# One pool of 62 operand tiles in place of three, and two plain tiles in place of a double one

## The chip, the cores and the metric

The kernel runs on one core of a Trainium2 chip. The metric is the device time of one execution in microseconds (us), lower is better. The core has five engines with a queue each, which run their instructions in order and wait for one another through semaphores: TensorE (PE in the rows, its weight loads PEld), VectorE (DVE), ScalarE (ACT), GpSimd (POOL) and SyncE (SP), which issues most of the loads.

## The reference

A conformer-like block and then two recurrent layers, on one sequence of 512 positions and 1024 channels, in float32:

```python
def first_block(x, ...):
    h = h + 0.5 * swiglu(rms_norm(h, ffn1_norm), ...)       # D_FF = 2816
    u = rms_norm(h, mix_norm); z = u @ w_in
    ya = neighbourhood_attention_2d(qa, ka, va, na_rpb)      # 8 heads of 64
    yb = windowed_gqa_sink(rope(qb), rope(kb), vb, sink)     # 8 heads, 2 for keys and values
    merged = sigmoid(ga) * (ya @ w_branch_a) + sigmoid(gb) * (yb @ w_branch_b)
    h = h + merged @ w_out
    h = h + 0.5 * swiglu(rms_norm(h, ffn2_norm), ...)
    return rms_norm(h, final_norm)

def second_block(x, ...):
    x = x + mlstm_mixer(rmsnorm(x, ln_g[0]), ...)   # 4 heads, causal convolution of 4 taps, output gate
    x = x + rglru_mixer(rmsnorm(x, ln_g[1]), ...)   # width 1536, convolution, gates in 8 blocks, scan
    return rmsnorm(x, final_g)
```

## The kernel before, in words

Channels lie on the 128 partitions and the 512 positions along the free axis, so the state is eight tiles `h` of 128x512. Every float32 matrix is split into a rounded part `hi` and a rest `lo`, and a product is three matmuls into one PSUM bank: hi by hi, hi by lo, lo by hi (`mm3`, L113 to L115). Weights are loaded by `wload`: SP loads `raw`, ScalarE casts it to `hi` (L98), VectorE subtracts to `lo` (L100); five `hi` and five `lo` tiles rotate, so a cast waits until TensorE has done with an older weight. Activations are split by `split` (ScalarE L122, VectorE L124) and the normalised inputs by `operand` (L139, L140).

The stages run one after the other: feed-forward 1, the mixer with its two attentions, feed-forward 2, the mLSTM, the RG-LRU and the last norm. At the start of most stages `opening` makes groups of 24 matmuls from the operands while `sumsq` squares the state on ScalarE (L157) and adds the squares on VectorE (L166); `rstd` (L178, L179) and `rows` (L185, L187) make the row of factors `rb` from it, with which VectorE scales what leaves PSUM (`silu2` L202 and L203, for one).

In the feed-forward, 18 of 22 pairs of hidden blocks go through `pair_products`, a scheme with seven products of half size for a 2 by 2 block product. It gathers its four quarters of 256 columns in a double tile `t` of 128x1024 (L325 to L337), then makes silu times product (L339, L340) and splits it. `xhalves` prepares the sums of the operands, in four steps.

In the mLSTM, for each of four heads, `x_proj` projects and scales, `conv` (L1006, L1009 three times) is followed by silu (L811) and a split, in `x_conv`; `o_proj` makes four groups at once in all four `bank` tiles, which ScalarE empties with a tanh into four `ctile`s (L869); `qk_proj` makes four more groups in `bank` tiles, emptied by L851 and L852. Head 0 also has `gate_rows` (L749 to L784) and `residual` (eight L789 on VectorE, with the row from L187). `scores` begins with four transposes (L878).

In the RG-LRU, four parts of three tiles: `x_proj` (L1043 and a convolution each), `gates` (six groups of 6 or 9 matmuls in `cbank` tiles, emptied by L1065 on ScalarE), `recur` (ScalarE L1076, L1077, L1080 with table loads between; VectorE L1084 to L1088; a split) and `out_proj` (L1096), in an order written at the end of `rglru`.

That order of calls is the program's. The framework's scheduler reorders each engine's instructions by priorities (`tc.high_priority`, with 100 for what empties PSUM and 75 for weights) and by when tiles of a pool are to be had. A pool has a fixed number of buffers under a tag: 40 tiles "act" of 128x512, 18 tiles "chain" (`ctile`) and 2 double tiles "four" in SBUF; 4 "bank" and 4 "cbank" in PSUM. A tile waits for the release of an older one when its pool has none left. The double tiles also hold the rope tables, two gates (`room`) and the `hi` parts of `qk_proj`.

Of the kernel before, what the change touches and what calls it, by code (L numbers as in the profile page):

```python
# [8 lines left out]
F32 = mybir.dt.float32  # L9
F32R = mybir.dt.float32r  # L10
# [4 lines left out]
P = 128  # L15
T = 512
# [26 lines left out]
def kernel(ctx: ExitStack, tc: tile.TileContext, a, out):  # L43
# [2 lines left out]

    cp = ctx.enter_context(tc.tile_pool(name="cp", bufs=1))
    op = ctx.enter_context(tc.tile_pool(name="op", bufs=1))
    ap = ctx.enter_context(tc.tile_pool(name="ap", bufs=40))
    wp = ctx.enter_context(tc.tile_pool(name="wp", bufs=5))  # L50
    sp = ctx.enter_context(tc.tile_pool(name="sp", bufs=32))
    gp = ctx.enter_context(tc.tile_pool(name="gp", bufs=2))
    hp = ctx.enter_context(tc.tile_pool(name="hp", bufs=KD))
    rp = ctx.enter_context(tc.tile_pool(name="rp", bufs=2))
    xp = ctx.enter_context(tc.tile_pool(name="xp", bufs=18))
    vp = ctx.enter_context(tc.tile_pool(name="vp", bufs=5))
    pp = ctx.enter_context(tc.tile_pool(name="pp", bufs=4, space=PSUM))
    qp = ctx.enter_context(tc.tile_pool(name="qp", bufs=4, space=PSUM))
# [1 line left out]
    def act_tile(dt=F32):  # L60
        return ap.tile([P, T], dt, tag="act", name="act")
# [2 lines left out]
        return pp.tile([P, T], F32, tag="bank", name="bank")  # L64

    def ctile(dt=F32):
        return xp.tile([P, T], dt, tag="chain", name="chain")

    def cbank():
        return qp.tile([P, T], F32, tag="cbank", name="cbank")  # L70
# [234 lines left out]
    def pair_products(pair, b, nxt, between):  # L305
        w = pair.w
        if nxt:
            nxt.load()
        m = bank()
        product(m[:, L], w["a11"], b["b11"])  # L310
        p1 = ctile()
        with tc.high_priority(offset=EVAC):
            S.copy(p1[:, L], m[:, L])
        c1, c2 = cbank(), cbank()
        product(c1[:, L], w["a12"], b["b21"])
        if nxt:
            nxt.first()
        between(0)
        product(c2[:, L], w["s1"], b["t1"])
        product(c2[:, R], w["s3"], b["t3"])  # L320
        product(c1[:, R], w["s2"], b["t2"])
        t = gp.tile([P, 2 * T], F32, tag="four", name="four")
        v = act_tile()
        with tc.high_priority(offset=EVAC):
            V.tensor_tensor(quarters(t)[:, 0:4:3], quarters(c1), twice(p1[:, L]), op=ALU.add)  # L325
            V.tensor_tensor(quarters(v), quarters(c2), twice(t[:, 3 * HT :]), op=ALU.add)
            V.scalar_tensor_tensor(t[:, 3 * HT :], c2[:, R], 1.0, v[:, L], op0=ALU.mult, op1=ALU.add)
        between(1)
        c3 = bank()
        product(c3[:, L], w["s4"], b["b22"])  # L330
        if nxt:
            nxt.sums()
        product(c3[:, R], w["a22"], b["t4"])
        if nxt:
            nxt.last()
        with tc.high_priority(offset=EVAC):
            V.tensor_tensor(t[:, HT : 3 * HT], c3, v, op=ALU.add)  # L337
        g, u = t[:, :T], t[:, T:]
        S.activation(g, g, AF.Silu)  # L339
        V.scalar_tensor_tensor(u, u, -1.0, g, op0=ALU.mult, op1=ALU.mult)  # L340
        return split(u)

    def ffn(x, gain, gu, dn, pre=None):
        xs = operand(x, gain)
        pre = pre or [wload(gu[0])]
        ws = pre
        pre, _, rb = opening(lambda n: group(ws[n] if n < len(ws) else wload(gu[n]), xs, (bank if n < 2 else cbank)()), x)

        def plain(j):
            pg, pu = pre[2 * j : 2 * j + 2] if j < 2 else [group(wload(gu[2 * j + i]), xs) for i in range(2)]  # L350
            s = silu2(pg, rb)
            u = act_tile()
            with tc.high_priority(offset=EVAC):
                V.tensor_tensor(u, pu, rb, op=ALU.mult)
            V.tensor_tensor(u, u, s, op=ALU.mult)
            return split(u)

        def down(o, w, base, us):
            ps = group(w, us, base=base)
            with tc.high_priority(offset=EVAC):  # L360
                V.scalar_tensor_tensor(x[o], ps, 0.5, x[o], op0=ALU.mult, op1=ALU.add)

        def down_two(o, k0):
            c = slice(k0 * P, k0 * P + T)
            with tc.high_priority(offset=BOOST):
                raw = raw_load([dn[o][:, c], dn[o + 1][:, c]], None)
                return wsplit(raw)

        b, step = xhalves(x, gain, rb)
        pr = [plain(0), plain(1)]  # L370
        for k in range(4):
            step(k)
        pr += [plain(2), plain(3)]
        def down_job(j):

            if j >= 20:
                return lambda i: None
            o, got, us = 2 * (j % 4), [], old

            def step(i):  # L380
                if i < 0:
                    got.append(down_two(o, 4 * (j // 4 - 1)))
                else:
                    down(o + i, got[0], 4 * i, us)

            return step

        cur = Pair(gu[8], gu[9])
        cur.load()
        cur.first()  # L390
        cur.sums()
        cur.last()
        old, new = pr, []
        for j in range(4, KF):
            nxt = Pair(gu[2 * j + 2], gu[2 * j + 3]) if j + 1 < KF else None
            job = down_job(j)
            job(-1)
            new.append(pair_products(cur, b, nxt, job))
            cur = nxt
            if j % 4 == 3 and j < 19:  # L400
                old, new = new, []
        for o in range(KD):
            dw = wload(dn[o][:, 16 * P :], 6 * P)
            down(o, dw, 0, new)
# [4 lines left out]
    def mixer(x):  # L409
# [32 lines left out]
        rope_t = {}  # L442

        def rope_tables():
            both = gp.tile([P, 2 * T], F32, tag="four", name="four")
            for i in range(2):
                t = both[:, i * T : (i + 1) * T]
                S.dma_start(t, a["rope"][i])
                rope_t[i] = t

# [29 lines left out]
            S.copy(vb, pv)  # L480
            bv.append(vb)

        room = []

        def gate(i):
            ps = group(wload(win[i]), xs)
            if i < 20:
                if not room:
                    room.append(gp.tile([P, 2 * T], F32, tag="four", name="four"))
                g = room[0][:, (i - 18) * T : (i - 17) * T]  # L490
            else:
                g = act_tile()
            with tc.high_priority(offset=EVAC):
                V.tensor_tensor(g, ps, rb, op=ALU.mult)
            S.activation(g, g, AF.Tanh, scale=0.5)
            return g
# [211 lines left out]
    def mlstm(x):  # L708
# [128 lines left out]
        def qk_proj(hd):  # L837
            xcs = st[hd].pop("xcs")
            qk = []
            for i in range(2):  # L840
                w = wload(a["mh"][hd][12 + i])
                w3 = tuple(z.rearrange("p (k m) -> p k m", k=4) for z in w)
                both = gp.tile([P, 2 * T], F32R, tag="four", name="four")
                for m in range(2):
                    ps = bank()
                    for k in range(4):
                        mm3(ps, tuple(z[:, k, m * P : (m + 1) * P] for z in w3), xcs[k], k == 0, k == 3)
                    hi, lo = both[:, m * T : (m + 1) * T], act_tile(F32R)
                    scale = (1.0 / 16, 1.0)[i]
                    with tc.high_priority(offset=EVAC):  # L850
                        S.activation(hi, ps, AF.Copy, scale=scale)  # L851
# [416 lines left out]
```

## Time and profile before

| | us |
|---|---|
| three runs | 1811.58, 1811.38, 1811.50 (median 1811.5) |
| the profiled execution | 1811.49 |
| its span | 1809.8 |
| TensorE busy (x9640) | 1786.7, 99% |
| VectorE busy (x1985) | 1244.5, 69% |
| ScalarE busy (x1205) | 813.6, 45% |
| GpSimd busy (x89) | 65.6, 4% |

The span runs from the first to the last instruction of the profile; what the execution's own time has beyond it lies around it. The granted clock of TensorE stands at nine tenths or more in all 40 slices. Busy time of 99% says that TensorE rarely had nothing in it; matmuls are pipelined, so one of 512 columns is shown with 0.39 us although the next starts 0.23 us later.

### The profile page before, as it was taken

What the parts mean: (1) busy time and instruction counts of PE and PEld (TensorE: products, weight loads), DVE (VectorE), ACT (ScalarE), POOL (GpSimd) and SP (SyncE); (2) the same over time, 40 slices, a digit from 0 to 9 for tenths busy, and PEclk for the clock granted to TensorE, in tenths of its full rate; (3) what the DMA queues carried; (4) which work ended last, traced back from release to release, by engine and by line L of the source; (5) the groups of instructions that cost most, each with busy time, mean ns of one, the idle gap of its engine ahead of it and who ended that gap; (6) DMA issues with size and microseconds to landing.
All of it is one profiled execution on the core that took longest, in us unless ns stands there. A gap on an engine that the chain in (4) does not pass through costs nothing.

```text
span 1809.8 us, 24643 instructions
## 1 busy us (share of the span) xinstructions
PE 1786.7 (99%) x9640; PEld 1515.3 (84%) x9640; DVE 1244.5 (69%) x1985; ACT 813.6 (45%) x1205; POOL 65.6 (4%) x89
## 2 busy tenths in 40 slices
PE   8999999999999999999999999999999999999998
PEld 6899999887776688799999988888888888888886
DVE  7977777735656465887777766758366566777775
ACT  5443344524345433443444444535334444456662
POOL 1000000000000000010000000000000000000000
PEclk9999999999999999999999999999999999999999
DMA  7466554433322123265556432222222231322312
GB/s 230 116 165 156 149 155 131 139 105 97 102 82 70 47 94 105 69 176 151 153 152 155 118 109 89 71 93 94 77 93 87 70 105 59 102 91 87 99 61 73
DMA packets 74805, 198.10 MB, mean 109 GB/s; under 512 B 8000, under 2 KB 8128, under 8 KB 74688
## 3 DMA queue, kind: packets, MB, share of 16 engines
q1 hardware_dynamic: 63024, 174.35, 30.0%
q0 software_dynamic: 9792, 18.88, 6.5%
q10 hardware_dynamic: 1872, 3.29, 0.6%
q8 instruction: 76, 1.25, 0.3%
q14 instruction: 41, 0.34, 0.1%
HBM read 193.08 MB, written 2.10 MB: 108 GB/s over the span
## 4 chain that ended last, share of the span: by engine, by line
PE 80%; issue 13%; DVE 4%; ACT 1%; DMA 1%; SPq 0%; POOLq 0%; POOL 0%; ACTq 0%; DVEq 0%
PE bank L113 21%; PE bank L114 20%; PE bank L115 20%; PE cbank L113 5%; PE cbank L115 5%; PE cbank L114 5%; PE cbank L635 1%; PE cbank L603 1%; DVE chain L124 1%; PE cbank L909 1%; PE cbank L910 1%; PE cbank L911 1%; DVE act L273 1%; PE cbank L572 0%; PE cbank L942 0%
## 5 line engine op out<-in xcount | busy, mean ns | idle before, releaser
L113 PE MATMUL bank<-act,hi 128*128 128x512 f32 (+1 forms) x1648 | 615.2, 374 | 8.3 <-ACT act L139 7.0
L114 PE MATMUL bank<-act,hi 128*128 128x512 f32 (+1 forms) x1648 | 612.8, 373 | 1.1 <-DVE act L140 1.0
L115 PE MATMUL bank<-act,lo 128*128 128x512 f32 (+1 forms) x1648 | 611.5, 372 | 0.7 <-DVE lo L100 0.7
L98 ACT CAST hi<-raw 128x1024 fp32r<-128x1024 f32 (+2 forms) x210 | 212.3, 1014 | 424.6 <-PE bank L114 193.7
L113 PEld LDWEIGHTS bank<-act,hi 128*128 128x128 f32 x1648 | 310.7, 189 | 67.0 <-ACT act L139 7.0
L114 PEld LDWEIGHTS bank<-act,hi 128*128 128x128 f32 x1648 | 310.9, 189 | 56.4 <-DVE act L140 3.3
L115 PEld LDWEIGHTS bank<-act,lo 128*128 128x128 f32 x1648 | 310.9, 189 | 56.2 <-issue 1.9
L100 DVE TENSOR_TENSOR lo<-raw,hi 128x1024 fp32r<-128x1024 f32 (+2 forms) x210 | 246.6, 1176 | 100.6 <-ACT hi L98 99.7
L220 ACT CAST hi<-raw 128x1024 fp32r<-128x1024 f32 x140 | 146.2, 1050 | 232.0 <-PE cbank L114 107.8
L222 DVE TENSOR_TENSOR lo<-raw,hi 128x1024 fp32r<-128x1024 f32 x140 | 170.8, 1224 | 82.1 <-ACT hi L220 77.7
L113 PE MATMUL cbank<-chain,hi 128*128 128x256 f32 x432 | 122.3, 283 | 1.7 <-ACT hi L220 1.7
L115 PE MATMUL cbank<-chain,lo 128*128 128x256 f32 x432 | 122.3, 283 | 0.9 <-DVE lo L222 0.9
L114 PE MATMUL cbank<-chain,hi 128*128 128x256 f32 x432 | 122.2, 283 | 0.0
L113 PE MATMUL cbank<-act,hi 128*128 128x256 f32 (+1 forms) x264 | 88.2, 334 | 0.0
L114 PE MATMUL cbank<-act,hi 128*128 128x256 f32 (+1 forms) x264 | 87.6, 332 | 0.0
L115 PE MATMUL cbank<-act,lo 128*128 128x256 f32 (+1 forms) x264 | 87.5, 332 | 0.0
L113 PE MATMUL bank<-hi,act 128*128 128x512 f32 x224 | 87.5, 391 | 0.0
L115 PE MATMUL bank<-hi,act 128*128 128x512 f32 x224 | 87.5, 391 | 0.0
L114 PE MATMUL bank<-lo,act 128*128 128x512 f32 x224 | 87.2, 389 | 0.0
L113 PEld LDWEIGHTS cbank<-chain,hi 128*128 128x128 f32 x432 | 82.7, 192 | 3.5 <-ACT hi L220 2.1
L115 PEld LDWEIGHTS cbank<-chain,lo 128*128 128x128 f32 x432 | 82.7, 192 | 1.4 <-DVE lo L222 1.1
L114 PEld LDWEIGHTS cbank<-chain,hi 128*128 128x128 f32 x432 | 82.8, 192 | 1.2
(287 smaller groups left out, 2574.0 us busy)
## 6 DMA issues: line engine op xcount, KB each, us to landing
raw<-in_mh_dram SPq DMA_DIRECT2D x64, 512.0 KB, 3.4
raw<-in_gu_dram SPq DMA_DIRECT2D x52, 512.0 KB, 3.5
raw<-in_gu_dram SPq DMA_DIRECT2D x72, 256.0 KB, 2.9
raw<-in_gu_dram POOLq DMA_DIRECT2D x36, 512.0 KB, 6.0
raw<-in_win_dram SPq DMA_DIRECT2D x34, 512.0 KB, 3.5
raw<-in_dn_dram SPq DMA_DIRECT2D x64, 256.0 KB, 2.9
v<-in_gu_dram SPq DMA_DIRECT2D x36, 256.0 KB, 2.6
raw<-in_mo_dram SPq DMA_DIRECT2D x16, 512.0 KB, 3.4
```

The costliest lines, as they stand in the source:

```text
L98: S.copy(hi[:, :cols], raw[:, :cols])
L100: V.tensor_tensor(lo[:, :cols], raw[:, :cols], f(hi[:, :cols]), op=ALU.subtract)
L113: PE.matmul(ps, st[0], mv[0], start=start, stop=False)
L114: PE.matmul(ps, st[0], mv[1], start=False, stop=False)
L115: PE.matmul(ps, st[1], mv[0], start=False, stop=stop)
L124: V.tensor_tensor(lo, x, f(hi), op=ALU.subtract)
L220: S.copy(hi, raw)
L222: V.tensor_tensor(lo, raw, f(hi), op=ALU.subtract)
L273: V.scalar_tensor_tensor(t, x[i], gain[:, i : i + 1], rb, op0=ALU.mult, op1=ALU.mult)
L603: PE.matmul(ps[:, :n], bq[i][ro, nb * P : nb * P + P], bk[0][ro, b0 * P : b1 * P], start=True, stop=True)
L635: PE.matmul(po[64 * g : 64 * g + 64, :], bv[0][:, kb * P + 64 * g : kb * P + 64 * g + 64], ptc, start=kb == b0, stop=kb == b1 - 1)
L909: PE.matmul(ps[:, :n], wh, vh[:, c0:c1], start=s == 0, stop=False)
```

## The change

The pools "four" and "chain" are gone; `ctile` takes its tiles from "act", which has 62 buffers (40 + 18 + 2 double ones). `pair_products` writes into two plain tiles `one` and `two`: the strided write to quarters 0 and 3 becomes a plain one into `one`, the last add of 512 columns becomes two of 256, and the silu and the split move into a function `hidden`. The rope tables, the two gates and the `hi` parts of `qk_proj` are plain tiles.

```diff
-    ap = ctx.enter_context(tc.tile_pool(name="ap", bufs=40))
+    ap = ctx.enter_context(tc.tile_pool(name="ap", bufs=62))
-    gp = ctx.enter_context(tc.tile_pool(name="gp", bufs=2))
-    xp = ctx.enter_context(tc.tile_pool(name="xp", bufs=18))
...
     def ctile(dt=F32):
-        return xp.tile([P, T], dt, tag="chain", name="chain")
+        return ap.tile([P, T], dt, tag="act", name="chain")
...
-        t = gp.tile([P, 2 * T], F32, tag="four", name="four")
-        v = act_tile()
+        one, two, v = act_tile(), act_tile(), act_tile()
         with tc.high_priority(offset=EVAC):
-            V.tensor_tensor(quarters(t)[:, 0:4:3], quarters(c1), twice(p1[:, L]), op=ALU.add)
-            V.tensor_tensor(quarters(v), quarters(c2), twice(t[:, 3 * HT :]), op=ALU.add)
-            V.scalar_tensor_tensor(t[:, 3 * HT :], c2[:, R], 1.0, v[:, L], op0=ALU.mult, op1=ALU.add)
+            V.tensor_tensor(quarters(one), quarters(c1), twice(p1[:, L]), op=ALU.add)
+            V.tensor_tensor(quarters(v), quarters(c2), twice(one[:, R]), op=ALU.add)
+            V.scalar_tensor_tensor(two[:, R], c2[:, R], 1.0, v[:, L], op0=ALU.mult, op1=ALU.add)
...
-            V.tensor_tensor(t[:, HT : 3 * HT], c3, v, op=ALU.add)
-        g, u = t[:, :T], t[:, T:]
+            V.tensor_tensor(one[:, R], c3[:, L], v[:, L], op=ALU.add)
+            V.tensor_tensor(two[:, L], c3[:, R], v[:, R], op=ALU.add)
+        return one, two
+
+    def hidden(pair, b, nxt, between):
+        g, u = pair_products(pair, b, nxt, between)
         S.activation(g, g, AF.Silu)
...
-            new.append(pair_products(cur, b, nxt, job))
+            new.append(hidden(cur, b, nxt, job))
...
-            both = gp.tile([P, 2 * T], F32, tag="four", name="four")
             for i in range(2):
-                t = both[:, i * T : (i + 1) * T]
+                t = act_tile()
                 S.dma_start(t, a["rope"][i])
...
-                both = gp.tile([P, 2 * T], F32R, tag="four", name="four")
                 for m in range(2):
...
-                    hi, lo = both[:, m * T : (m + 1) * T], act_tile(F32R)
+                    hi, lo = act_tile(F32R), act_tile(F32R)
```

The change moves instructions, most of them in other functions than those it edits. Three places follow, each as the engine's order before and then in the changed kernel (a line is shown as line, operation, out<-in, shape; x4 is four alike in a row). The changed kernel's lines are lower: L861 is L869 of before, L804 L811, L120 L122, L936 L944, L843 L851, L96 L98, L1057 L1065, L1068 L1076, L1072 L1080, L201 L203, L164 L166, L1088 L1096, L1114 L1122, L176 L178.

ScalarE in head 0 of the mLSTM, before: silu (L811) and split (L122) of the second to fourth convolution, with the four tanh of o_proj (L869).

```order
L811 ACTIVATE act<-act 128x512
L98 CAST hi<-raw 128x1024
L122 CAST act<-act 128x512
L869 ACTIVATE chain<-bank,small 128x512 x2
L944 ACTIVATE act<-act,skq 128x512
L869 ACTIVATE chain<-bank,small 128x512 x2
L811 ACTIVATE act<-act 128x512
L98 CAST hi<-raw 128x1024
L122 CAST act<-act 128x512
L944 ACTIVATE act<-act,skq 128x512
L811 ACTIVATE act<-act 128x512
L122 CAST act<-act 128x512
```

The same in the changed kernel:

```order
L804 ACTIVATE act<-act 128x512
L120 CAST act<-act 128x512
L936 ACTIVATE act<-act,skq 128x512
L804 ACTIVATE act<-act 128x512
L120 CAST act<-act 128x512
L936 ACTIVATE act<-act,skq 128x512
L804 ACTIVATE act<-act 128x512
L120 CAST act<-act 128x512
L861 ACTIVATE chain<-bank,small 128x512 x4
L936 ACTIVATE act<-act,skq 128x512
L843 ACTIVATE act<-bank 128x512
```

The four tanh that stood behind the second split stand behind the fourth. In head 3 they move in the same way, from around the third split to behind the fourth; in heads 1 and 2 they stay.

ScalarE in the RG-LRU, before: from the last L1065 of the first gates through the first recurrence.

```order
L1065 ACTIVATE chain<-cbank,small 128x512
L1076 ACT_TABLE_LOAD
L1076 ACTIVATE chain<-chain,small 128x512 x2
L1077 ACTIVATE chain<-chain,small 128x512 x2
L1076 ACTIVATE chain<-chain,small 128x512
L203 ACT_TABLE_LOAD
L203 ACTIVATE act<-act 128x512
L1077 ACTIVATE chain<-chain,small 128x512
L1080 ACT_TABLE_LOAD
L1080 ACTIVATE chain<-chain 128x512 x3
```

The same in the changed kernel:

```order
L1057 ACTIVATE chain<-cbank,small 128x512
L96 CAST hi<-raw 128x1024
L201 ACTIVATE act<-act 128x512
L96 CAST hi<-raw 128x896
L201 ACTIVATE act<-act 128x512
L96 CAST hi<-raw 128x896
L1068 ACT_TABLE_LOAD
L1068 ACTIVATE chain<-chain,small 128x512
L201 ACT_TABLE_LOAD
L201 ACTIVATE act<-act 128x512
```

Three weight casts and two silu stand ahead of the recurrence now. Further on, the L1065 of the second gates stand behind the three splits of the next convolutions, and on TensorE the last 15 matmuls of those gates behind 90 of the following groups.

VectorE at the end of the kernel, before: L1096 empties the last groups, L1122 scales the state, L166 adds squares, L178 begins the last norm.

```order
L1122 TENSOR_SCALAR act<-h,vec 128x512
L166 TENSOR_TENSOR chain<-chain 128x512
L1096 SCALAR_TENSOR_TENSOR h<-bank,h 128x512
L1122 TENSOR_SCALAR act<-h,vec 128x512
L166 TENSOR_TENSOR chain<-chain 128x512
L1096 SCALAR_TENSOR_TENSOR h<-bank,h 128x512
L1122 TENSOR_SCALAR act<-h,vec 128x512
L178 TENSOR_SCALAR small<-cbank 128x4
```

The same in the changed kernel:

```order
L1114 TENSOR_SCALAR act<-h,vec 128x512
L1088 SCALAR_TENSOR_TENSOR h<-bank,h 128x512
L1114 TENSOR_SCALAR act<-h,vec 128x512
L1088 SCALAR_TENSOR_TENSOR h<-bank,h 128x512
L1114 TENSOR_SCALAR act<-h,vec 128x512
L164 TENSOR_TENSOR chain<-chain 128x512 x6
L176 TENSOR_SCALAR small<-cbank 128x4
```

The six adds that stood one by one between the L1096 now stand together behind the last L1122.

## Rows read from the trace of the kernel before

**Rows 1.** What TensorE waited for, whole span: total us, times, longest.
```profile
PE bank L113 <- ACT act L139: 7.0, 1, 7.0
...
PE bank L478 <- DVE act L475: 1.6, 1, 1.6
PE bank L114 <- DVE act L140: 1.0, 3, 0.5
```

**Rows 2.** Busy us (PE, PEld, DVE, ACT, POOL), PEclk, DMA share, GB/s: pair loops.
```profile
75.00:345.00 270.00, 270.00 (x1861) 252.20 (x1861) 207.25 (x267) 112.95 (x147) 18.11 (x15) 1.00 0.58 154
```

**Rows 3.** Groups by line and shape, VectorE, 100 to 330 us: busy, mean ns.
```profile
L337 DVE TENSOR_TENSOR four<-bank,act 128x512 f32<-128x512 f32 x16 | 10.9, 684 | 0.0
...
L327 DVE SCALAR_TENSOR_TENSOR four<-cbank,act 128x256 f32<-128x256 f32 x16 | 6.8, 424 | 0.5
```

**Rows 4.** Timeline, TensorE, qk_proj of head 0: start, length, then idle before.
```profile
1133.19 0.60 PE L185 MATMUL cbank<-ident,small 128*128 128x128 f32 x4
...
1143.03 1.21 PE L113 MATMUL bank<-act,hi 128*128 128x512 f32 x4 [0.49 <-ACT act L122]
...
1146.63 0.68 PE L113 MATMUL cbank<-four 128*128 128x512 f32 x2 [0.28 <-ACT four L851]
```

**Rows 5.** Timeline, ScalarE, the same place.
```profile
1129.43 0.69 ACT L869 ACTIVATE chain<-bank,small 128x512 f32<-128x512 f32 x1
...
1141.69 0.63 ACT L811 ACTIVATE act<-act 128x512 f32<-128x512 f32 x1 [3.70 <-DVE act L1009]
```

**Rows 6.** Timeline, VectorE, the same place.
```profile
1133.83 0.69 DVE L187 COPY rb<-cbank 128x512 f32<-128x512 f32 x1
1134.56 2.08 DVE L789 SCALAR_TENSOR_TENSOR h<-h,vec,rb 128x512 f32<-128x512 f32 x3
1136.55 0.68 DVE L124 TENSOR_TENSOR act<-act 128x512 fp32r<-128x512 f32 x1
1137.15 0.54 DVE L1006 TENSOR_SCALAR act<-act,vec 128x512 f32<-128x512 f32 x1
...
1145.29 1.21 DVE L100 TENSOR_TENSOR lo<-raw,hi 128x1024 fp32r<-128x1024 f32 x1
```

**Rows 7.** Timelines of VectorE, ScalarE and TensorE, head 3.
```profile
1490.21 2.32 DVE L1009 SCALAR_TENSOR_TENSOR act<-act,vec 128x511 f32<-128x511 f32 x3
...
1493.95 0.62 ACT L122 CAST act<-act 128x512 fp32r<-128x512 f32 x1
...
1491.57 0.39 PE L113 MATMUL bank<-act,hi 128*128 128x512 f32 x1
```

**Rows 8.** Timelines of ScalarE and (last two rows) TensorE, RG-LRU.
```profile
1621.30 1.28 ACT L1076 ACT_TABLE_LOAD   x1
...
1635.92 0.95 ACT L98 CAST hi<-raw 128x896 fp32r<-128x896 f32 x1 [0.33 <-PE bank L114]
...
1662.76 0.68 ACT L1065 ACTIVATE chain<-cbank,small 128x512 f32<-128x512 f32 x1
...
1666.30 0.62 ACT L122 CAST act<-act 128x512 fp32r<-128x512 f32 x1 [0.72 <-DVE act L1009]
...
1687.33 0.62 ACT L122 CAST act<-chain 128x512 fp32r<-128x512 f32 x1 [2.09 <-DVE chain L1088]
...
1658.38 0.39 PE L113 MATMUL cbank<-act,hi 128*128 128x512 f32 x1
...
1700.55 0.39 PE L113 MATMUL cbank<-act,hi 128*128 128x512 f32 x1
```

**Rows 9.** Timelines of VectorE and (third row) TensorE at the end.
```profile
1793.91 0.69 DVE L166 TENSOR_TENSOR chain<-chain 128x512 f32<-128x512 f32 x1 [0.18 <-ACT chain L157]
...
1797.33 0.49 DVE L1122 TENSOR_SCALAR act<-h,vec 128x512 f32<-128x512 f32 x1
...
1798.02 0.38 PE L173 MATMUL cbank<-ones,chain 128*128 128x1 f32 x2
...
1799.78 0.16 DVE L178 TENSOR_SCALAR small<-cbank 128x4 f32<-128x4 f32 x1 [1.96 <-PE cbank L173]
```

More of the change, by code (lines that the diff above doesn't have):

```diff
@@ L481, in vb_group @@
             bv.append(vb)
-        room = []
         def gate(i):
             ps = group(wload(win[i]), xs)
[L487 to L492, printed above, removed]
+            g = act_tile()
             with tc.high_priority(offset=EVAC):
```

## The prediction

> **What bounds the kernel now.** I read the page's busy shares first (TensorE 99%), then the table of what the idle TensorE waited for, then the busy time of one stretch, then timelines of the places where the order of instructions differs. Lines are those of the kernel before; in the changed kernel the same code stands 2 lower up to the feed-forward and 7 or 8 lower from the mLSTM on (L869 is its L861).
>
> What idles TensorE is short: 7.0 us once, at the start, for the first operand L139, 1.0 us for its partner L140, 1.6 us in the mixer for L475 [rows 1]. In the pair loops of the first feed-forward it is busy 270.00 of 270 us at clock 1.00 [rows 2]. So the change cannot save more than a few us, and everything hangs on whether it opens new gaps. Its arithmetic is the same but for one add. What moves is order: the pools decide when a tile is to be had, and with it where the scheduler puts an instruction. I went through each engine's new order and looked for an instruction that TensorE waits for and that now stands behind slower work.
>
> **The split add.** L337 wrote 512 columns in 0.684 us; now two adds write 256 each. The nearest row of 256 columns took 0.424 us [rows 3]: +0.16 us a pair, 5.9 us over 36 pairs, all VectorE's. It costs nothing, because the matmuls of the pair loop cover it, as [rows 2] shows; with that cover gone it would be at most those 5.9 us. The Trainium skill (VectorE: DVE Perf Modes, section on the TRN2 errata) asks for tiles of at least 512 elements so that a fixed latency is paid once, which speaks against this edit; the rows agree in direction (0.848 against 0.684 us). By that rule alone the sum would be 5.9 us higher; by the rows TensorE sees none of it.
>
> **The openings** (first feed-forward, second feed-forward). All eight operand pairs L139/L140 now stand ahead of the squares L157 and adds L166. This can return the 1.0 us of waits for L140 and a little of the 7.0. Against it, the sum of squares ends later: six adds at up to 0.69 us [rows 9], 4.1 us, and behind them stand the evacuations L202 and the steps of xhalves; but two groups of 24 matmuls lie ahead of the sum on TensorE. I take +1, over both, nearer to none than to all of it; ends -2 and +4. **The mixer**: L475 moves ahead of two instructions of VectorE, so up to 1.6 us of [rows 1] can go; I take -1, ends -1.6 and 0. Attention scores also move by some tens of matmuls; 0, ends -2 and +2.
>
> **mLSTM, head 0: the main term.** o_proj fills all four `bank` tiles; L869 on ScalarE empties them, and qk_proj's first matmul needs one. Before, the first L869 started at 1129.43, ahead of the third and fourth convolution's activation (the fourth L811 at 1141.69, which waited 3.70 us for VectorE) [rows 5], and TensorE went on behind the four transposes of 1133.19 without a gap; it later waited 0.49 and 0.28 us [rows 4]. Now the four L869 stand behind the fourth L811 and L122. That one waits for the last L1009 on VectorE, whose convolutions are themselves later, as the gate rows (L749 to L784), delayed too, stand ahead of them. Counting VectorE's new list from L187, which TensorE's own transposes release at 1133.83 as before: 8 L789 and 7 L1009 at 0.66 us (three L789 fill 1134.56 to 1136.55), 2 L124 at 0.60, 2 L1006 at 0.5, one L100 at 1.2 [rows 6] = 9.9 + 1.2 + 1.0 + 1.2 = 13.3, from 1134.56 to 1147.9. Then L811, L122 and L869, 0.63 + 0.62 + 0.69 [rows 5, 7]: the first bank is free near 1149.8. TensorE, which has only four more transposes to do first (four took 0.60 us), arrives near 1134.1. That is a wait of 15.7 us. Since TensorE's queue runs in order, all later matmuls wait with it (on ScalarE only L944 and the four L851, which follow those matmuls anyway, queue behind L869); the operands are then ready, so the 0.77 us of [rows 4] falls away: +14.9 at most. The 48 matmuls run a little denser in one stretch; I take **+14.5**, ends 11 and 16.
>
> **Head 3.** The same move: the L869 now follow the fourth L122. Here VectorE's convolution is not delayed; its L1009 end at 1490.21 + 2.32 = 1492.5, and L811, L122, L869 add 1.94, so a bank is free at 1494.5; from L122's old start, 1493.95, it would be 1495.3. TensorE wants it at 1491.57 [rows 7], plus 0.5 for transposes brought forward: **+2.7**, ends 2 and 3.5. Heads 1 and 2 keep their order.
>
> **RG-LRU.** L1076, the head of a recurrence on ScalarE, ran at 1621.30. It now stands behind three more weight casts, the last of which TensorE releases only at 1635.92 [rows 8]: 14.6 us later. VectorE's part of that recurrence moves with it, and behind that stand the evacuations and convolutions of the next block, whose last L122 was at 1666.30. Part of the delay is VectorE's idle time; I take 11 us of it, so 1677.5. The gates' L1065 now stand behind that L122, one table load later, near 1679.3; TensorE has moved the last 15 matmuls of these gates, at 1658.38, back behind 90 others; at 0.227 us each (186 matmuls lie between 1658.38 and 1700.55) it comes to them, and wants the first bank, at 1678.8: a wait of 0.5 us, and with L1065's own 0.7 us, 1.2. From the last L1065 (1662.76) to the last output of the recurrence (L122 at 1687.33) took 24.6 us [rows 8]. That L1065 now waits for the 15 matmuls, near 1683.6, and the chain ends at 1706.5 to 1708. Its reader, out_proj, is moved up to where the next block's 15 gate matmuls stood, 1700.55; with the wait before it starts at 1701.8 and reaches that operand 15 matmuls, 3.4 us, later, at 1705.2: another wait of 1.3 to 3 us; I take 3, as the cast's partner L124 comes after it. Two further recurrences follow in the same kind of order; 1.8 us for both. **+6**, ends 0 (the cover holds) and +10.
>
> **The tail.** Six L166 adds of the last sum of squares ran one by one between L1096s, the last at 1793.91. Now all six stand behind the last L1122, which ends at 1797.82. A chain of six at 0.6 to 0.69 us ends near 1801.6; the matmuls of the sum stood at 1798.02 and L178 behind them at 1799.78 [rows 9]. Half of the transposes get done meanwhile. **+3.5**, ends 2.5 and 4. The same six adds move at the opening of RG-LRU; there 48 matmuls cover them.
>
> **Queues.** Weight loads on SP and the loads on POOL keep their order but for three; ScalarE's rope loads go to two plain tiles. Nothing waits on them: 0.
>
> **Sum.** 1 - 1 + 14.5 + 2.7 + 6 + 3.5 = 26.7 us, added to the profiled execution's 1811.49 us: **1838.2 us**. That execution stands at the median of the three runs, 1811.5.
>
> **The rivals.**
> *RG-LRU's cover holds.* The 24.6 us recurrence was 20 us early before, and my waits there are differences of two long chains. Without them: 1832.2 us. Chance 0.20.
> *More of the same.* Every wait near its upper end (+4 openings, +16, +3.5, +10, +4, less 1): about 1848 us. For it speaks that a late convolution makes every later evacuation late. Chance 0.10.
> *The evacuations cost nothing.* Four groups rotate through four banks, and if the last convolution of a head were done before TensorE comes for a bank, L869 and L1065 behind it would be hidden. The point is whether the fourth L1009 ends by about 1132. Then only the tail's 3.5 remains, less 3 gained at openings and L475: 1812 us, no difference. Against it: L187 alone starts at 1133.83, and 13.3 us of counted work stand between it and that L1009 [rows 6]. Chance 0.07. The Trainium skill (Perfetto Trace Analysis, section Matmuls) says that groups rotating through banks let the evacuation of one overlap the next group's matmuls; by that rule this rival is what happens, and [rows 4, 5] of the kernel before agree with it, as long as L869 runs at once.
> *The change does nothing.* The gaps were never set by pools and the new order hides as well as the old: 1811.5 us. Chance 0.03.
>
> **How the numbers follow.** The forecast has 0.60. A measurement of this kernel can tell about 0.2%, 3.6 us, from no change. The forecast and the first two rivals are slower, 0.90; of the last two 0.08 fall within 0.2% and 0.02 are faster. The ends of the terms add up to +10 and +40. Eight in ten lie between 1823 us (RG-LRU at 0 and nearly every other term at its lower end) and 1848 us (the second rival); what is left out is mostly the last two rivals.
>
> **What would show it.** In the new profile: one idle time of TensorE of 11 to 16 us in qk_proj of head 0, put down to ScalarE's L861; a second of 2 to 3.5 us in head 3; short ones in RG-LRU on L1057 and on the splits of the recurrence; L176 about 3.5 us further from the last matmul of out_proj; none in the pair loops. Wrong: if head 0 has no idle time over 5 us, the main term falls; if gaps appear in the pair loops, the split add was not covered.

## The result and the profile after

The changed kernel takes **1863.9 us** (median of 4 runs, 1861.9 to 1864.8) against 1811.5 (1811.4 to 1812.0): ratio 1.0287, 95% interval 1.0269 to 1.0305. That is 52.4 us slower, where 26.7 was forecast, and 16 us above the upper end of the range. The direction and the main place were right, the size was not.

The page of the changed kernel (its profiled execution took 1863.89 us): the span, the busy time of TensorE and VectorE, and the granted clock.

```profile
span 1862.1 us, 24738 instructions
...
PE 1804.3 (97%) x9640; PEld 1529.2 (82%) x9640; DVE 1252.9 (67%) x2021; ACT 816.7 (44%) x1205; POOL 67.2 (4%) x89
...
PEclk9999999999999999999999998999999999999998
```

TensorE has the same 9640 instructions in both kernels, so its lost time can be placed: what it waited for, over the whole span (total us, times, longest; eight rows of 0.7 us or less are not shown).

```profile
PE bank L111 <- ACT chain L861: 18.7, 2, 16.2
PE bank L111 <- ACT act L137: 6.8, 1, 6.8
PE bank L111 <- ACT act L120: 4.4, 2, 2.7
PE cbank L111 <- ACT act L120: 4.2, 2, 2.1
PE cbank L169 <- DVE chain L164: 3.9, 1, 3.9
PE bank L111 <- DVE h L1088: 2.6, 1, 2.6
PE cbank L111 <- ACT chain L120: 1.8, 2, 0.9
PE bank L112 <- DVE act L122: 1.1, 2, 0.9
PE cbank L169 <- DVE chain L161: 1.0, 1, 1.0
PE cbank L902 <- DVE act L825: 0.9, 1, 0.9
PE cbank L111 <- ACT chain L1057: 0.8, 1, 0.8
PE bank L478 <- DVE act L475: 0.7, 1, 0.7
```

The 7.0 us of L139 and the 1.6 of L475 [rows 1] are still there in part (6.8 and 0.7); nearly all the rest is new. All rows of the table, the eight that are not shown included, add up to 50.7 us, those of the kernel before to 14.6. So 36.1 us of the loss are idle time. The other part stands in no table of waits; the granted clock shows it. Busy time by stretch of 4 us (PE, PEld, DVE, ACT, POOL, then PEclk, DMA share, GB/s), around the 16.2 us:

```profile
1143.00:1147.00 4.00, 0.57 (x6) 0.32 (x3) 4.00 (x7) 2.02 (x3) 0.00 (x0) 1.00 0.00 0
1147.00:1151.00 4.00, 0.00 (x0) 0.00 (x0) 4.00 (x7) 0.72 (x1) 0.00 (x0) 0.55 0.00 0
1151.00:1155.00 4.00, 0.00 (x0) 0.00 (x0) 4.00 (x7) 1.25 (x2) 0.00 (x0) 0.50 0.00 0
...
1159.00:1163.00 4.00, 3.18 (x8) 2.52 (x9) 0.69 (x1) 3.10 (x6) 0.00 (x0) 0.50 0.00 0
1163.00:1167.00 4.00, 4.00 (x16) 3.27 (x15) 0.69 (x1) 0.60 (x1) 0.00 (x0) 0.81 0.00 0
```

While TensorE idles the clock goes from 1.00 (2.4 GHz) to 0.50 (1.2 GHz), and TensorE begins its work at 0.50 when it goes on. The timeline of TensorE at this place:

```profile
1142.53 0.60 PE L183 MATMUL cbank<-ident,small 128*128 128x128 f32 x4
1142.96 0.60 PE L870 MATMUL cbank<-ident,cT 128*128 128x128 f32 x4
1159.82 0.80 PE L111 MATMUL bank<-act,hi 128*128 128x512 f32 x1 [16.25 <-ACT chain L861]
...
1160.84 0.63 PE L113 MATMUL bank<-act,lo 128*128 128x512 f32 x1
1161.26 0.63 PE L111 MATMUL bank<-act,hi 128*128 128x512 f32 x1
1161.69 0.63 PE L112 MATMUL bank<-act,hi 128*128 128x512 f32 x1
...
1164.25 0.51 PE L112 MATMUL bank<-act,hi 128*128 128x512 f32 x1
```

From the second on, matmuls of 512 columns start 0.42 to 0.43 us apart here, not 0.227. From 1159.82 to 1164.25 there are ten, in 4.43 us instead of 2.27: 2.2 us on top of the wait.

Where the loss lies, stage by stage, comes from setting the start of TensorE's k-th instruction in one trace against that of the k-th in the other: how much the lag grows over a stage, in us. The stretches are in the time of the kernel before. A lag comes from one execution of each kernel, the profiled one.

| stretch | stage | lag | new idle time in it |
|---|---|---|---|
| to 75 | opening, feed-forward 1 | +4.3 | 1.5 |
| 75 to 345 | its pair loops | +0.1 | 0 |
| 345 to 640 | mixer | -1.7 | 0.1 |
| 640 to 800 | opening, feed-forward 2 | +3.0 | 1.3 |
| 800 to 1070 | its pair loops and end | +0.8 | 0 |
| 1070 to 1120 | mLSTM, opening and gate rows | +2.8 | 1.3 |
| 1120 to 1180 | mLSTM, head 0 | +18.4 | 16.7 |
| 1480 to 1560 | mLSTM, head 3 | +5.5 | 2.9 |
| 1560 to 1790 | RG-LRU | +12.7 | 8.4 |
| 1790 to the end | tail | +7.4 | 3.9 |

Heads 1 and 2 give 0.1. The sum is 53.4 at TensorE's last instruction; the spans differ by 52.3, as what follows that instruction is a little shorter. By the trace's record of the granted clock, TensorE was busy for 33.7 us at 0.50, behind waits in eight places of the changed kernel, and for none in the kernel before. If that work takes half the time at 1.00, which is an estimate from the 0.42 to 0.43 us above against 0.227, the lower clock cost 16.8 us. That is nearly all of the 17.3 us by which the lag (53.4) exceeds the new idle time (36.1). The mixer is an exception: it became 1.7 us shorter with no less idle time, and why was not followed.

### The profile page after: what moved, and what is told of

It reads as the page before. It is cut to its first block, busy times and chain, and to the rows that moved or that the text cites. A ratio compares the mean times of both kernels' runs of the same rounds, so it can differ in the third digit from the quotient of the medians.

```text
span 1862.1 us, 24738 instructions
## 1 busy us (share of the span) xinstructions
PE 1804.3 (97%) x9640; PEld 1529.2 (82%) x9640; DVE 1252.9 (67%) x2021; ACT 816.7 (44%) x1205; POOL 67.2 (4%) x89
## 4 chain that ended last, share of the span: by engine, by line
PE 77%; issue 14%; DVE 5%; ACT 2%; DMA 0%; POOL 0%; SPq 0%; POOLq 0%; ACTq 0%; DVEq 0%
PE bank L111 20%; PE bank L112 19%; PE bank L113 19%; PE cbank L111 5%; PE cbank L112 4%; PE cbank L113 4%; PE cbank L628 1%; DVE lo L220 1%; PE cbank L596 1%; PE cbank L902 1%; PE cbank L903 1%; PE cbank L565 0%; PE cbank L901 0%; DVE act L271 0%; DVE chain L122 0%
## 5 line engine op out<-in xcount | busy, mean ns | idle before, releaser
L96 ACT CAST hi<-raw 128x1024 fp32r<-128x1024 f32 (+2 forms) x210 | 211.9, 1014 | 427.8 <-PE bank L112 176.9
L98 DVE TENSOR_TENSOR lo<-raw,hi 128x1024 fp32r<-128x1024 f32 (+2 forms) x210 | 246.6, 1176 | 79.9 <-ACT hi L96 78.6
L120 ACT CAST act<-act 128x512 fp32r<-128x512 f32 x104 | 64.5, 620 | 73.1 <-DVE act L341 34.2
L122 DVE TENSOR_TENSOR act<-act 128x512 fp32r<-128x512 f32 x104 | 71.7, 689 | 32.3 <-ACT act L120 32.1
L111 PEld LDWEIGHTS cbank<-chain,hi 128*128 128x128 f32 x432 | 83.9, 195 | 3.5 <-ACT chain L120 2.2
```

The lines of the kernel that those rows point to most:

```text
L96: S.copy(hi[:, :cols], raw[:, :cols])
L98: V.tensor_tensor(lo[:, :cols], raw[:, :cols], f(hi[:, :cols]), op=ALU.subtract)
L111: PE.matmul(ps, st[0], mv[0], start=start, stop=False)
L120: S.copy(hi, x)
L122: V.tensor_tensor(lo, x, f(hi), op=ALU.subtract)
```

## The experiments

Theory A says that tiles of one tag are given out in the order in which the program asks for them. While `ctile` had a tag of its own, its requests didn't stand in line behind those for `act` tiles; now each does, and with it the instruction that writes the tile. Theory B says that 62 tiles are too few. A third possibility is the plain tiles and the split add. In the kernels of the experiments most lines stand one lower than in the changed one (L862 is its L861).

### 1 and 2: which half of the change it is

The first kernel has the plain tiles without the merged pool, the second the merged pool without the plain tiles:

```diff
 e1_plain_tiles, against the changed kernel
-    ap = ctx.enter_context(tc.tile_pool(name="ap", bufs=62))
+    ap = ctx.enter_context(tc.tile_pool(name="ap", bufs=44))
+    xp = ctx.enter_context(tc.tile_pool(name="xp", bufs=18))
     def ctile(dt=F32):
-        return ap.tile([P, T], dt, tag="act", name="chain")
+        return xp.tile([P, T], dt, tag="chain", name="chain")
 e2_merge_only, against the kernel before
-    ap = ctx.enter_context(tc.tile_pool(name="ap", bufs=40))
+    ap = ctx.enter_context(tc.tile_pool(name="ap", bufs=58))
-    xp = ctx.enter_context(tc.tile_pool(name="xp", bufs=18))
-        return xp.tile([P, T], dt, tag="chain", name="chain")
+        return ap.tile([P, T], dt, tag="act", name="chain")
```

> The change's plain tiles and split add, but squares, tanh outputs and all other chain tiles back in a pool of 18 of their own (44 act tiles, 18 chain tiles). If the shared tag is what costs: within 3 us of the kernel before, 1808.5 to 1814.5 us. If the split add or the plain tiles cost something: 1820 us or more, up to the changed kernel's 1864.

> Kernel before with chain tiles taken from the act pool (58 tiles), the two double tiles and the single wide add kept. If the shared tag is what costs: 1855 to 1870 us, as the changed kernel. If the plain tiles cost: near 1811.5 us.

Measured: the first 1811.9 us, ratio 1.0002 [0.9993, 1.0011]; the second 1862.9 us, ratio 1.0285 [1.0268, 1.0302]. The whole loss comes from the shared tag, none of it from the plain tiles. The first also speaks against theory B: it has the same 62 tiles as the changed kernel, only under two tags.

### 3 and 4: one user taken back out of the shared tag

```diff
 e3_square_pool, against the changed kernel (bufs of ap: 58)
+    qs = ctx.enter_context(tc.tile_pool(name="qs", bufs=4))
-            sq = ctile()
+            sq = qs.tile([P, T], F32, tag="sq", name="sq")
-                t = ctile() if perm else sq
+                t = qs.tile([P, T], F32, tag="sq", name="sq") if perm else sq
 e4_o_pool, against the changed kernel (bufs of ap: 54)
+    os = ctx.enter_context(tc.tile_pool(name="os", bufs=8))
-                t = ctile()
+                t = os.tile([P, T], F32, tag="o", name="o")
```

> Changed kernel, with only the squares of the sums of squares in four tiles of their own (58 act tiles, the total unchanged). If a shared tag forces squares behind operands, the waits of the openings of feed-forward 1 and 2 and of the mLSTM and of the tail go. Counting waits alone (about 8 us more than in the kernel before): 1856 us. Counting also the slower matmuls that follow each wait while the granted clock is low (5.2, 2.9, 2.9 and 7.4 us lost at the four places): 1845.5 us. If instead 62 tiles are too few: no change, 1864 us, or slower.

> Changed kernel, with only the four tanh outputs of o_proj in a pool of eight of their own (54 act tiles, the total unchanged). If the shared tag forces the tanh behind the convolutions: the waits of 16.3 and 2.5 us in heads 0 and 3 go. Waits alone: 1846 us; with the slower matmuls behind them 1841 us. If 62 tiles are too few: no change or slower, 1864 us or more.

Measured: 1854.0 us, ratio 1.0237 [1.0222, 1.0252], and 1855.6 us, ratio 1.0248 [1.0232, 1.0263]. Both are faster than the changed kernel with fewer tiles in the shared tag.

With the squares out, the tail's 7.4 us go to 0.0 and the stage 1070 to 1120 from 2.8 to 0.4. The two openings of the feed-forward keep their loss (3.5 and 3.1); there I had the wrong user, and the forecast of that run, 1845.5 us with the clock counted, was 8.5 us too low. That the other one, 1856 us from waits alone, came close is luck: it too had counted on the openings.

With the four tanh outputs out, head 3's loss falls from 5.5 to 1.3, but head 0 keeps 13.7 of 18.4. The wait for the tanh (L862 there) is gone; others have its place (TensorE's waits, 1130 to 1200 us of that kernel):

```profile
PE bank L112 <- ACT act L121: 4.6, 2, 3.6
PE cbank L902 <- DVE chain L886: 3.1, 1, 3.1
```

In head 0 the convolutions themselves are late. So in head 0 two causes cover each other, and taking one away gives little back; the forecasts, 1846 and 1841 us, were 9.6 and 14.6 us too low.

### 5 to 11: one user put into the shared tag

From here the first experiment's kernel is the base (44 `act` and 18 `chain` tiles, 1811.9 us), and single users of `ctile` move to `act`:

```diff
 c1_squares
-            sq = ctile()
+            sq = act_tile()
-                t = ctile() if perm else sq
+                t = act_tile() if perm else sq
 c2_o: in o_proj
-                t = ctile()
+                t = act_tile()
 c3_halves: in xhalves
-            t12, t34 = ctile(), ctile()
+            t12, t34 = act_tile(), act_tile()
 c9_ffn: c3_halves and
-                pr = split(t, ctile)
+                pr = split(t)
-        p1 = ctile()
+        p1 = act_tile()
 c10_ffn_sq: c9_ffn and c1_squares
 c6_o_rows: c2_o and, in gate_rows,
-            return ctile()[R, :]
+            return act_tile()[R, :]
-            t = ctile()
+            t = act_tile()
 c5_gates: in gates and recur
-                    th = ctile()
+                    th = act_tile()
-                av = ctile()
+                av = act_tile()
```

> The converse of the third experiment. Its kernel is the first one (plain tiles, a pool of 44 act tiles and a pool of 18 chain tiles; 1811.9 us) with one edit: the squares of sumsq and the tiles they are added into come from the tag act. By the theory (a tile stands behind all earlier requests of its own tag, and TensorE pays each wait and then some us at the lower granted clock) the losses of the squares come back, and they alone: 2.1 us at the opening of the mLSTM and 7.4 us at the tail, 9.5 in all, 1821.4 us. If waits alone counted: 1.0 + 3.9, 1816.8 us. If the loss came from too few tiles in one big pool, the chain pool now has room and act has 44 instead of 62: then either nothing (1812) or losses in stages without squares, the heads of the mLSTM first.

> The converse of the fourth experiment: the first kernel (1811.9 us) with one edit, the four tanh outputs of o_proj come from the tag act. Theory: the tanh stand behind the last convolution again in heads 0 and 3. Head 3 loses its 5.4 us; head 0 loses less than the 17.6 of the changed kernel, since its gate rows stay early and VectorE's convolutions with them: 10 to 15 us. Sum 15 to 20, 1827 to 1832 us. Rival (too few tiles): no such wait, 1812 us. Nothing elsewhere.

> The first kernel (1811.9 us) with one edit: the two sums t12 and t34 of each step of xhalves come from the tag act. Theory: the openings of the two feed-forwards lose what they lose in the changed kernel, 4.7 and 2.9 us there, with part of the wait of the second perhaps hidden: 5 to 8 us, 1817 to 1820 us, with TensorE waiting for the splits. If the openings' loss needs the late squares as well: 1812 to 1814 us.

> The first kernel (1811.9 us) with one edit: the gates and decays of the RG-LRU (the tanh outputs and the exponential's tile) come from the tag act. Theory: the 12.7 us that the changed kernel loses between 1660 and 1790 come back, and nothing else: 1824.6 us; waits alone, 8.4 us, 1820.3. If those losses were handed down from earlier stages or came from a pool that is too small: no change, 1812 us.

> The first kernel (44 act tiles, 18 chain tiles; 1811.9 us) with three edits in the feed-forward: t12, t34, their splits and the copy p1 of pair_products all come from act; t12 and t34 alone changed nothing. If the openings' loss is that of the feed-forward's own tiles in the shared tag: 3.5 to 4.7 us at the first and 2.9 us at the second opening, 1818 to 1820 us. If the splits wait behind squares or behind tiles of other stages: 1812 us. With only 44 tiles in act the pair loops may open gaps too; then the sum is above 1820 and the gaps stand between 75 and 345 and between 775 and 1050.

> The kernel of c9_ffn with one more edit: the squares of sumsq come from act as well. If the two losses add up: the 8.0 us of c1_squares on top of c9_ffn. If the openings of the feed-forwards need both together: c9_ffn at 1812 and this one at 1825 to 1830 us, with 4.7 and 2.9 us at the openings, 2.1 us at the opening of the mLSTM and 6 to 7 us at the tail.

> The kernel of c2_o (tanh outputs in act, 1824.7 us, 10.0 us lost in head 0) with one more edit: the gate rows of head 0 and their sums come from act as well. The prediction held that late gate rows make VectorE's convolutions late and with them the wait in head 0. If so, head 0 loses 15 to 18 us as in the changed kernel (18.4), and the sum is 1830 to 1833 us. If the rows cost nothing by themselves: 1824.7 us again. Head 3 as in c2_o, 2.5 us, or 5.4 us if the lower granted clock comes behind its wait.

Measured (us, ratio to the kernel before with its 95% interval), and the lag by stage as in the table above. The profiled execution of c1_squares (1821.6 us) and of c5_gates (1844.5 us) was the slowest of its kernel, 1.8 us above the median, so their lags add up to more than the medians differ.

| | us | ratio | to 75 | 345 to 640 | 640 to 800 | 1070 to 1120 | head 0 | head 3 | RG-LRU | tail |
|---|---|---|---|---|---|---|---|---|---|---|
| changed kernel | 1863.9 | 1.0287 [1.0269, 1.0305] | 4.3 | -1.7 | 3.0 | 2.8 | 18.4 | 5.5 | 12.7 | 7.4 |
| e1_plain_tiles | 1811.9 | 1.0002 [0.9993, 1.0011] | -0.2 | 0.2 | 0.0 | 0.0 | 0.7 | 0.0 | 0.0 | 0.0 |
| c1_squares | 1819.8 | 1.0044 [1.0030, 1.0058] | 1.5 | -0.1 | 0.1 | 2.1 | 0.8 | 0.0 | 0.0 | 6.4 |
| c2_o | 1824.7 | 1.0072 [1.0057, 1.0087] | 0.2 | -0.2 | 0.1 | 0.0 | 10.0 | 2.5 | 0.0 | 0.0 |
| c6_o_rows | 1835.8 | 1.0129 [1.0114, 1.0144] | 1.0 | 0.0 | 0.0 | 0.7 | 20.3 | 2.5 | 0.0 | 0.0 |
| c3_halves | 1811.0 | 0.9998 [0.9988, 1.0007] | -0.3 | -0.3 | -0.6 | 0.0 | 0.7 | 0.0 | 0.0 | 0.0 |
| c9_ffn | 1819.2 | 1.0038 [1.0025, 1.0051] | 3.3 | -0.2 | 4.1 | 0.0 | 0.7 | 0.0 | 0.0 | 0.0 |
| c10_ffn_sq | 1829.6 | 1.0094 [1.0077, 1.0111] | 3.9 | 1.7 | 4.4 | 0.9 | 0.7 | 0.0 | 0.0 | 6.8 |
| c5_gates | 1842.8 | 1.0172 [1.0157, 1.0187] | -0.1 | 1.9 | 0.0 | 0.0 | 0.7 | 0.0 | 30.4 | 0.0 |

Nothing but the tag changes in these edits, and the order changes with it: with the tanh in `act`, ScalarE's four tanh of head 0 move from behind the second split to behind the fourth; with the squares in `act`, all eight squares stand behind all eight operands of an opening instead of among them. Set against e1_plain_tiles, the order of instructions on ScalarE, VectorE and TensorE changes only where the moved tiles are used: in c2_o in heads 0 and 3 alone, in c5_gates in RG-LRU alone. Each user loses time in those stages, and (but for a few us at the start and in the mixer) nowhere else. The 1.9 us of c5_gates in the mixer come with an unchanged order: the wait for L475 is 2.1 us there, 1.8 in e1_plain_tiles, and the clock is at 0.50 behind it; in c10_ffn_sq it is the same with 2.0 us. All this is what theory A says, though the order in which tiles are given out is itself inferred from the order of the instructions. The losses of the changed kernel can be looked for one by one:

- *Squares* (c1_squares): the opening of the mLSTM and the tail, as expected, within 2 us of the sum. On top of c9_ffn the squares cost 10.4 us (c10_ffn_sq), where 8.0 were expected; the mixer's 1.7 is part of that.
- *Tanh outputs and gate rows*: the tanh alone cost 10.0 in head 0, with the gate rows 20.3, more than the 15 to 18 expected. In head 3 they cost 2.5, not the 5.4 expected of c2_o (the last section has the clock there). The prediction's chain (late gate rows, hence late convolutions, hence a later tanh behind the last of them) is confirmed by that second step. In c6_o_rows the wait is even longer than in the changed kernel:

```profile
PE bank L112 <- ACT act L862: 21.5, 2, 19.1
```

- *Feed-forward*: t12 and t34 alone do nothing, a miss of 5 to 8 us; with their splits and p1 the openings lose 3.3 and 4.1. Which of the two it is was not tried. The pair loops of the first feed-forward stay full even with 44 `act` tiles (a stretch of c9_ffn, columns as above):

```profile
75.00:345.00 270.00, 270.00 (x1868) 252.31 (x1867) 207.16 (x285) 112.95 (x146) 18.10 (x15) 1.00 0.55 150
```

- *Gates*: a miss. 12.7 us were expected back, 30.4 came. TensorE's waits in c5_gates, 1650 to 1825 us:

```profile
PE bank L112 <- ACT act L121: 9.2, 3, 7.6
PE bank L112 <- DVE h L1089: 6.3, 3, 3.6
PE bank L113 <- DVE act L123: 4.5, 2, 3.8
```

They are the waits of the changed kernel in this stage (splits, evacuations of out_proj), two to four times as long. Here the number of tiles may count beside the order: 44 `act` tiles lose 30.4 us, while the kernels with 54 (e4_o_pool), 58 (e2_merge_only) and 62 lose 13.2, 12.7 and 12.7. Between 54 and 62 the number does nothing here: throughout this stage (1620 to 1845 us of the changed kernel) these three have the same order of instructions on ScalarE, VectorE and TensorE. At 44 it is not shown, as c5_gates also has fewer users in `act`, and no run has the changed kernel's users with 44 tiles. Whether more than 62 would lose less was not tried.

### 12: the gates taken back out

```diff
 d7_gates, against the changed kernel
-    ap = ctx.enter_context(tc.tile_pool(name="ap", bufs=62))
+    ap = ctx.enter_context(tc.tile_pool(name="ap", bufs=53))
+    tg = ctx.enter_context(tc.tile_pool(name="tg", bufs=9))
-                    th = ctile()
+                    th = tg.tile([P, T], F32, tag="th", name="th")
-                av = ctile()
+                av = tg.tile([P, T], F32, tag="th", name="th")
```

> The changed kernel with one edit: the gates and decays of the RG-LRU (the tanh outputs and the exponential's tile) come from a pool of their own with 9 tiles, and act shrinks from 62 to 53. The converse run lost 31 us there with 44 tiles in act, where the changed kernel with 62 loses 12.7 us, so in this stage the number of tiles may count beside the order in which they are given out. If order within one tag is what counts: the 12.7 us between 1660 and 1790 go, 1851 us. If the number counts as much: act with 53 loses more than with 62, 1864 to 1880 us. Everything before 1660 as in the changed kernel (about 34 us).

Measured: 1852.7 us, ratio 1.0222 [1.0207, 1.0237]. RG-LRU's lag is 0.0 instead of 12.7, with nine tiles fewer in `act`; the mixer loses 3.9 us more than in the changed kernel and the tail 1.1 less, so that the sum missed by 1.7. In the changed kernel it is the common line, not the number of tiles, that costs RG-LRU its time.

In the mixer the number does count. Neither the gates nor the tanh outputs are used there, so d7_gates and e4_o_pool differ from the changed kernel in that stage only by the tiles that `act` lacks; yet the order of instructions changes between 520 and 640 us, and the lag goes from -1.7 with 62 tiles to -0.3 with 54 (e4_o_pool) and 2.2 with 53 (d7_gates). Both have a new wait for L488, of 1.8 and 2.5 us.

No version beat the kernel before: c3_halves at 0.9998 [0.9988, 1.0007] can't be told from it.

## Why the prediction was half right

**Right: the split add.** Two adds of 0.417 and 0.414 us stand for the one of 0.684 [rows 3], 0.15 us more a pair (groups of VectorE, 100 to 330 us: line, busy us, mean ns):

```profile
L334 DVE TENSOR_TENSOR act<-bank,act 128x256 f32<-128x256 f32 x15 | 6.3, 417 | 0.0
L335 DVE TENSOR_TENSOR act<-bank,act 128x256 f32<-128x256 f32 x15 | 6.2, 414 | 0.0
```

TensorE is busy for all of the pair loops, as in [rows 2], and e1_plain_tiles costs nothing (the changed kernel, columns as there):

```profile
75.00:345.00 270.00, 270.00 (x1869) 252.34 (x1868) 206.47 (x284) 111.60 (x143) 18.11 (x15) 1.00 0.56 150
```

The rule on tiles of at least 512 elements (the Trainium skill, VectorE: DVE Perf Modes, section on the TRN2 errata) shows in the rows of L334 and L335 and not in the time.

**Right: head 0's wait, its cause and its length.** Forecast 15.7 us, measured 16.25. TensorE comes to the place 9.34 us late (L183 at 1142.53, 1133.19 in [rows 4]). Less this, the first bank came at 1150.5; 1149.8 was forecast. The timelines of ScalarE and then VectorE show the chain, the tanh behind the fourth split, which waits for the last L1001, among eight L782:

```profile
1157.90 0.63 ACT L804 ACTIVATE act<-act 128x512 f32<-128x512 f32 x1 [2.09 <-DVE act L1001]
1158.56 0.62 ACT L120 CAST act<-act 128x512 fp32r<-128x512 f32 x1
1159.08 2.41 ACT L861 ACTIVATE chain<-bank,small 128x512 f32<-128x512 f32 x4
```

```profile
1144.89 2.07 DVE L782 SCALAR_TENSOR_TENSOR h<-h,vec,rb 128x512 f32<-128x512 f32 x3
...
1155.54 2.32 DVE L1001 SCALAR_TENSOR_TENSOR act<-act,vec 128x511 f32<-128x511 f32 x3
```

The banks rotate as before, and TensorE still waits 16.25 us, because the evacuation L861 stands last among these rows of ScalarE; so the third rival did not come about. The Trainium skill's rule behind that rival (Perfetto Trace Analysis, section Matmuls: groups rotating through PSUM banks overlap their evacuation) does not hold at this place.

**Right: L475 and head 3's wait.** L475 went from 1.6 to 0.7 (-0.9, forecast -1); head 3's wait for L861 was 2.47 us, forecast 2.7. The mixer's term as a whole was right by luck: new waits of 0.7 us (for L555) and 0.2 (for L625) used up what L475 gave back.

**Wrong: "+14.5", "+2.7", "+6", "+3.5" as the whole cost of a wait.** The step that failed is the sum: it added each wait at its own length and let the matmuls behind it run at 0.227 us. Of the lag, 53.4 - 36.1 = 17.3 us is no idle time. By the estimate above, 16.8 us of this is TensorE at the lower granted clock (over the span the mean granted clock fell from 0.998 to 0.985); the prediction had no term for it. The tail shows it most, first TensorE's timeline, then the stretches:

```profile
1842.41 2.13 PE L1122 MATMUL bank<-ident,act 128*128 128x128 f32 x16
1848.46 0.58 PE L169 MATMUL cbank<-ones,chain 128*128 128x1 f32 x2 [3.92 <-DVE chain L164]
...
1851.90 3.65 PE L1122 MATMUL cbank<-ident,act 128*128 128x128 f32 x16
```

```profile
1845.00:1849.00 4.00, 0.54 (x3) 0.54 (x3) 3.00 (x5) 0.00 (x0) 0.00 (x0) 0.77 0.00 0
1849.00:1853.00 4.00, 4.00 (x21) 4.00 (x21) 0.16 (x1) 0.00 (x0) 0.69 (x1) 0.50 0.02 4
```

The wait of 3.92 us was forecast as 3.5. Behind it the matmuls of the sum and the last 16 transposes run at 0.50: the sixteen take 3.65 us, and 2.13 just before the wait. The stage lost 7.4. The Trainium skill (TensorE: Matmul & The Clock Gate, section on HAM oscillation) counts this penalty on top of the wait; the rows agree.

**Wrong: "other" terms taken near zero.** The rest of the miss, 36.1 - 26.7 = 9.4 us, is idle time that was sized too small:
- "+1" for the openings: 1.5 + 1.3 us of new idle time, 7.3 us of lag. The steps of xhalves were named as being late, but their splits were not followed to TensorE, which waits 2.1 us for one L120 in each opening.
- "mLSTM opening", not costed: 1.0 us for L161, 0.4 and 0.3 for the gate rows. "There 48 matmuls cover them" was said of RG-LRU's opening and held there: no wait for L164 or L161 shows in it.
- RG-LRU's "1.8 for both" later recurrences: 2.6 us for L1088 and 2.7 for a split. VectorE's evacuation of out_proj (L1088) now stands behind the scans of a recurrence, the same pattern as in head 0. The two terms that were worked out were near: L1065, now L1057, 0.84 (1.2 forecast) and the splits at out_proj 2.75 (3).
- The mixer's -1: 0.1 us of new idle time.
- Head 0: 16.7 us of new idle time for 14.5. The 0.9 us of L902 for L825 were not foreseen, and the deduction for a denser stretch did not come.

**The range.** Its upper end was the second rival, nearly every wait near its upper end. It could not hold a cost that came behind most of the longer waits and was in no term.

## What to carry to other kernels

Pools under separate tags are more than memory: here each tag behaved as a line of its own in which tiles are given out, and merging them put short-lived results behind earlier requests, even with the total number of tiles unchanged. Where an engine's new order is known, look for evacuations that now stand behind a long chain on their engine, in every stage, and price a new wait of TensorE as its length at the lower end of a range and, at the upper end, with the matmuls behind it at the lower clock. Undoing one of two late inputs shows little: move each cause alone into a kernel that has none, and then a second beside it. The sizes found there need not carry over: the gates cost 30.4 us in such a kernel and 12.7 in the changed one.

## What the runs showed of the hardware

A wait of the same length did not always bring the lower clock. In head 3 TensorE waits 2.47 us for the tanh both in the changed kernel and in c2_o. In the first the clock stands at 0.50 afterwards, in the second it stays at 1.00, and the stage loses 5.5 us against 2.5 (stretches of the changed kernel, then of c2_o):

```profile
1522.00:1524.00 2.00, 1.57 (x5) 1.23 (x6) 0.52 (x1) 2.00 (x5) 0.00 (x0) 0.72 0.40 127
1524.00:1526.00 2.00, 2.00 (x6) 1.62 (x5) 0.00 (x0) 0.72 (x2) 0.00 (x0) 0.50 0.36 143
```

```profile
1504.00:1506.00 2.00, 1.22 (x5) 1.03 (x6) 2.00 (x6) 2.00 (x5) 0.00 (x0) 1.00 0.28 49
1506.00:1508.00 2.00, 2.00 (x10) 1.62 (x10) 0.05 (x1) 1.97 (x3) 0.00 (x0) 1.00 0.55 221
```

The same 2.47 us stand in four more kernels: the clock fell to 0.50 in e2_merge_only, e3_square_pool and d7_gates (5.4 to 5.5 us of lag) and stayed at 1.00 in c6_o_rows (2.5). Nor did the longer wait always cost more clock: in the changed kernel the 2.74 us for a split in RG-LRU left it at 1.00 (1818 to 1820 us), while behind the 1.03 us for L161 in the opening of the mLSTM it stood at 0.51 (1084 to 1086 us). What decides it stays open.
